# Three of the four sums of down-projection weight blocks made during the up stage, and weight loads counted in buffers (hybrid decoder layer, one core)

## The chip, the cores and the metric

One core of a Trainium2 chip runs the kernel. The metric is the device time of one execution in microseconds (us); the median of 3 runs stands for a kernel. The engines are called TensorE (PE, matmuls; PEld is its weight load), VectorE (DVE), ScalarE (ACT), GpSimd (POOL) and SyncE (SP, which issues transfers). A transfer that adds into its destination (an accumulate) is issued by GpSimd.

## The reference, cut to what matters

One decoder layer on 512 tokens of width 1024, in float32: attention and a gated short convolution, merged and projected, and then a feed-forward part. Only the last line concerns the change:

```python
x = x + mixed @ w_out
h = rms_norm(x, norm2_g)
return x + jnp.square(jax.nn.relu(h @ w_up)) @ w_down     # w_up 1024 x 4096, w_down 4096 x 1024
```

## The kernel before

Every weight comes from DRAM in blocks of 128 x 1024 (512 KB). `Weights` holds a plan of them in the order of use. Each block is split into a high and a low part (ScalarE copies into `w_hi`, line 87; VectorE subtracts into `w_lo`, line 89), in four steps of half a block's high, half a block's low, and again. Each product is then three matmuls (`mm3`, lines 252 to 254): high by high, low by high, high by low. The splits are put into the program a few blocks ahead of their use: `split_step` is called between matmuls, two blocks ahead in an up stage and three in a down stage. There are 3 buffers for raw blocks (`w_raw`) and 4 for split ones. SyncE, which issues the loads (line 65), works in program order: a load whose buffer is still read holds up all loads behind it. `load_to(self.ns + 2)` runs after each split and loads up to the plan's second entry after the next.

The feed-forward part runs in four groups of 1024 inner channels. An up stage computes 8 tiles of 128 channels by 512 tokens (8 x 24 matmuls) and squares them (`act_evac`, lines 881 to 903: ScalarE 888 and 895, VectorE 889 and 896 to 902). A down stage (`st_down`, lines 931 to 990) multiplies them by the group's part of `w_down` with seven products of halves in place of eight (Strassen's scheme in Winograd's form). The scheme needs blocks of `w_down` and sums of them; block (kh, nh) is row half kh and column half nh, each in two pieces c = 0 and 1 of 512 KB:

| product | weights, in order of use | where they lie before |
|---|---|---|
| 1 | (0,0) | staged tile `st_a` |
| 2 | (1,0) | `w_raw` |
| 3 | (0,0) + (0,1) | `st_a` after an accumulate |
| 4 | (1,1) + (0,0) + (0,1) | staged tile `st_e` |
| 5 | (1,1) | `w_raw` |
| 6 | (0,1) + (1,1) | staged tile `st_b` |
| 7 | the 4th + (1,0) | `st_e` after another accumulate |

So a down stage has 14 chunks (7 products by 2 pieces) of 12 matmuls, 4 splits steps of a later block between them. After the second piece of a product VectorE adds its accumulators into `x1` (line 941); where the next product accumulates in the same PSUM tile, TensorE waits for that add. A plan entry is a DRAM block, or a pair of functions: one that gives a staged tile, and one that is called after its split and issues what comes next for that tile: a load of the next group's block (SyncE, line 142) or an accumulate (GpSimd, line 146). In the order before:

- after the split of `st_a` as (0,0): accumulate (0,1) onto `st_a`, then accumulate `st_a` onto `st_e`;
- after its second split: load the next group's (0,0) into it, which has to wait until the accumulate that reads `st_a` has ended;
- after the first split of `st_e`: accumulate (1,0) onto it; after its second: load the next group's (1,1);
- after the split of `st_b`: load the next group's (0,1) and accumulate (1,1) onto it.

As pairs take up entries of the plan but no raw buffer, two entries ahead is often less than three loads ahead there. In the first up stage the tiles are loaded once, and `st_b` is accumulated (lines 914 to 916).

Of the kernel before, what the change touches and what calls it, by code (L numbers as in the profile page):

```python
# [6 lines left out]
F32 = mybir.dt.float32  # L7
F32R = mybir.dt.float32r
AF = mybir.ActivationFunctionType
ALU = mybir.AluOpType  # L10
# [3 lines left out]
P = 128  # L14
# [21 lines left out]
class Weights:  # L36
# [16 lines left out]
    def dram(self, n):  # L53

        src = self.flat[self.at : self.at + P * n].rearrange("(p n) -> p n", p=P)
        self.at += P * n
        return src

    def load_to(self, i):
        while self.nl <= min(i, len(self.plan) - 1):  # L60
# [5 lines left out]
                self.loaded[self.nl] = t[:, :n]  # L66
            self.nl += 1

    def split_step(self):

        nc, k = self.nc, self.ns
        if k >= len(self.plan):
            return
        e = self.plan[k]
        if self.step == 0:
            self.load_to(k)
            if isinstance(e, tuple):
                self.loaded[k] = e[0]()
            hi = self.hl.tile([P, WMAX], F32R, name="w_hi", tag="w_hi")
            lo = self.hl.tile([P, WMAX], F32R, name="w_lo", tag="w_lo")  # L80
            self.parts[k] = (hi, lo)
        hi, lo = self.parts[k]
        t = self.loaded[k]
        n = t.shape[1]
        v = slice(0, n // 2) if self.step < 2 else slice(n // 2, n)
        if self.step % 2 == 0:
            nc.scalar.activation(hi[:, v], t[:, v], AF.Copy)  # L87
        else:
            nc.vector.tensor_tensor(lo[:, v], t[:, v], hi[:, v].bitcast(F32), ALU.subtract)  # L89
        self.step = (self.step + 1) % 4  # L90
        if self.step == 0:
            self.loaded.pop(k)
            self.ns += 1
            if isinstance(e, tuple):
                e[1]()
            self.load_to(self.ns + 2)

    def split_to(self, i):
        while self.ns <= min(i, len(self.plan) - 1):
# [7 lines left out]
def layer(tc, flat, sizes, x, cst, wck, wcv, g1, g2, out):  # L107
    nc = tc.nc
# [25 lines left out]
    W.plan = [W.dram(n) for n in sizes]  # L134


    st = {}

    def st_load(g, what, c):
        src = {"a": (0, 0), "b": (0, 1), "e": (1, 1)}[what]  # L140
        t = st["pool"].tile([P, 1024], F32, name=f"st_{what}{c}", tag=f"{what}{c}")
        nc.sync.dma_start(t, down_src(g, *src, c))
        st[what, c] = t

    def st_add(t, src):
        nc.gpsimd.dma_start(t, src, accum_op=ALU.add)  # L146

    def st_loads(g, c, what):
        if g < 4:
            st_load(g, what, c)  # L150
            if what == "b":
                st_add(st["b", c], down_src(g, 1, 1, c))

    def down_src(g, kh, nh, c):
        return down_blocks[g][kh, nh][:, c * 1024 : (c + 1) * 1024]

    def st_plan(g):


        def first(c):  # L160
            st_add(st["a", c], down_src(g, 0, 1, c))
            st_add(st["e", c], st["a", c])

        def tile_of(what, c, done):
            return (lambda: st[what, c], done)

        def both(f):
            return [f(c) for c in range(2)]

        out = both(lambda c: tile_of("a", c, lambda: first(c)))  # L170
        out += both(lambda c: down_src(g, 1, 0, c))
        out += both(lambda c: tile_of("a", c, lambda: st_loads(g + 1, c, "a")))
        out += both(lambda c: tile_of("e", c, lambda: st_add(st["e", c], down_src(g, 1, 0, c))))
        out += both(lambda c: down_src(g, 1, 1, c))
        out += both(lambda c: tile_of("b", c, lambda: st_loads(g + 1, c, "b")))
        out += both(lambda c: tile_of("e", c, lambda: st_loads(g + 1, c, "e")))
        return out

    down_blocks = []
    for g in range(4):  # L180
        W.plan += [W.dram(1024) for _ in range(8)]
        down_blocks.append({(kh, nh): W.dram(2048) for kh in range(2) for nh in range(2)})
        W.plan += st_plan(g)
# [415 lines left out]
    def u_scores(u, c):  # L599

        h, br = units[u]
        n = P * (c + 1)
        a, b = (S - n, S + P) if c == 0 else (S, S + n) if br else (S - n, S)
        t = slice(c * P, (c + 1) * P)
        ps = ps_sc.tile([P, S], F32, name="sc", tag="sc")
        for k, ks in enumerate((KS1, KS2)):
            nc.tensor.matmul(  # L607
                ps[:, : b - a], QS[h][:, t], ks[h // 4][:, a:b], start=k == 0, stop=k == 1
            )

        def soft(v, src):
            p = p_of(v, c)
            mn, sm = (nst[:, v % 4, k, c : c + 1] for k in range(2))
            dd = C_DD + S - n if c == 0 or units[v][1] else C_DR
            nc.vector.tensor_tensor_reduce(
                p, src, cs[:, dd : dd + n], -(2.0 ** -(h + 1)), 3.0e38,
                op0=ALU.add, op1=ALU.min, accum_out=mn,
            )
            later(1, lambda: nc.scalar.activation(
                p, p, AF.Exp, scale=-1.0, bias=mn, accum_out=sm  # L620
            ))

        if c == 0:
            for k in range(2):
                soft(u + k, ps[:, k * P : (k + 1) * P])
        else:
            soft(u, ps[:, :n])

        def norm(c0):
            r = nst[:, u % 4, 1, c0 : c0 + 2]  # L630
            nc.vector.tensor_scalar(r, r, 1.0e-30, None, op0=ALU.max)
            nc.vector.reciprocal(r, r)
            nc.vector.tensor_tensor(r, r, gates[:, c0 : c0 + 2, (br + 1) * NH + h], ALU.mult)
            for k in (c0 + 1, c0):
                nc.gpsimd.tensor_scalar(
                    p_of(u, k), p_of(u, k), nst[:, u % 4, 1, k : k + 1], 1.0,
                    op0=ALU.mult, op1=ALU.mult,
                )

        if c == 2 or c == br:  # L640
            later(3, lambda: norm(2 if c == 2 else 0))
# [4 lines left out]
    def u_trans(u, grp):  # L646
        br = units[u][1]
        pth, ptl = ptb[u % 2]
        pt = ps_tr.tile([P, S], F32, name="ptu", tag="tr")
        n = 0  # L650
        for j in grp:
            for c in range(j, NT):
                k = j if br else c - j
                nc.tensor.transpose(  # L654
                    pt[:, n : n + P], p_of(u, c)[:, k * P : (k + 1) * P], ident
                )
                n += P
        at = slice(PT_AT[grp[0]], PT_AT[grp[0]] + n)
        nc.scalar.activation(pth[:, at], pt[:, :n], AF.Copy)
        later(1, lambda: nc.vector.tensor_tensor(  # L660
            ptl[:, at], pt[:, :n], pth[:, at].bitcast(F32), ALU.subtract
        ))

    def u_pv(u, js):
        h, br = units[u]
        g = h // 4
        pth, ptl = ptb[u % 2]
        if br == 0 and js[0] == 0:
            pv_now[0] = ps_pv.tile([P, S], F32, name="pv", tag="pv")
        pv = pv_now[0]  # L670
        for j in js:
            at, q0 = (0, 256) if j == 3 else (PT_AT[j], j * P)
            w = S - q0
            v = V[:, j, br * 2 + g, :, :].rearrange("p a d -> p (a d)")
            nc.tensor.matmul(  # L675
                pv[:, q0:], v, pth[:, at : at + w], start=(br == 0 and j == 0), stop=False
            )
            nc.tensor.matmul(  # L678
                pv[:HD, q0:], v[:, :HD], ptl[:, at : at + w], start=False, stop=False
            )  # L680
# [18 lines left out]
    for u in range(nu + 2):  # L699
        s = [lambda c=c, u=u: u_scores(u, c) for c in (3, 2, 1, 0)[: 4 - u % 2]] if u < nu else []  # L700
        t, f = [], []
        if 1 <= u <= nu:
            t = [lambda g=g, v=u - 1: u_trans(v, g) for g in ((3, 2), (1,), (0,))]
        if u >= 2:
            f = [lambda j=j, v=u - 2: u_pv(v, j) for j in ((0, 1), (2, 3))]
# [62 lines left out]
    for n in range(NKO):  # L768
        sg = []
        for i in range(2):  # L770
            ps = tile_t(ci, (xh, xl), NKO, ps_t)
            s = gp.tile([P, S], F32, name=f"sg{i}", tag=f"sg{i}")
# [138 lines left out]
        up.tile([P, NP, 7, 256], F32R, name="ul"),  # L911
        None,
    ]
    for c in range(2):
        for what in "abe":
            st_loads(0, c, what)
    pss = [ps_acc.tile([P, S], F32, name="acc", tag="acc") for _ in range(4)]
    for half in range(2):
        for f in range(4):
# [188 lines left out]
```

## Time and profile before

| | us |
|---|---|
| median of 3 runs | 868.86 (865.09 to 871.91) |
| the profiled execution | 869.74 |
| its span, first to last instruction | 868.0 |
| first up stage, up to its last matmul | 484 to 535 |
| the four down stages begin at | 535.1, 630.0, 725.8, 821.5 |

Times in the rows are us from the start of the span, with the length of a piece in the second column of a timeline; brackets hold the idle time of the engine just before an instruction and what ended it. Matmuls overlap, so the length of one is more than its share of the time. TensorE's granted clock is 1.00 at 2.4 GHz and 0.50 at 1.2 GHz.

### The profile page before, as it was taken

The numbers are of one execution on the slowest core, as the hardware profiler recorded it, in microseconds if no ns is written. First come the engines' busy times: TensorE is split into PE (matmuls) and PEld (weight loads), VectorE is DVE, ScalarE is ACT, GpSimd is POOL, SyncE is SP. The second block draws the span as 40 slices with busy tenths as digits, with TensorE's granted clock in tenths as the row PEclk, the third lists the DMA queues.
The fourth block names the chain that finished last, engine by engine and source line by source line (L and its number), as shares of the span: only waits on it lengthen the run. The fifth ranks groups of instructions, "written<-read, shape, count | busy, mean of one in ns | idle before, by whom it ended". The sixth has DMA issues, their size and how long they took to land.

```text
span 868.0 us, 10722 instructions
## 1 busy us (share of the span) xinstructions
PE 822.8 (95%) x3941; PEld 678.5 (78%) x3941; DVE 512.0 (59%) x1026; ACT 358.4 (41%) x735; POOL 91.8 (11%) x138
## 2 busy tenths in 40 slices
PE   5999999999999999999999998889998899889998
PEld 4898778888887888888888986668876787768876
DVE  6677977666665544333435566555665367455684
ACT  5455455545544423232324444233443244323451
POOL 0101642221221000000000001100010001100020
PEclk9999999999999999999999999989999999999999
DMA  8213121212121242323262563873176724782372
GB/s 318 83 52 122 49 73 49 74 49 74 52 70 41 82 134 85 105 89 97 98 243 72 188 177 51 187 220 107 66 145 193 220 72 74 170 265 98 73 164 79
DMA packets 29861, 101.17 MB, mean 117 GB/s; under 512 B 3441, under 2 KB 3825, under 8 KB 29809
## 3 DMA queue, kind: packets, MB, share of 16 engines
q1 hardware_dynamic: 24336, 81.02, 28.0%
q0 software_dynamic: 4608, 16.78, 10.6%
q10 hardware_dynamic: 864, 2.69, 0.9%
q8 instruction: 31, 0.51, 0.2%
q14 instruction: 22, 0.17, 0.1%
HBM read 94.18 MB, written 2.10 MB: 111 GB/s over the span
## 4 chain that ended last, share of the span: by engine, by line
PE 60%; issue 20%; DMA 9%; DVE 6%; ACT 3%; POOL 1%; SPq 0%; POOLq 0%; ACTq 0%; DVEq 0%
PE acc L252 16%; PE acc L254 16%; PE acc L253 16%; DMA w_raw<-w_flat 5%; DMA st_e<-st_a 2%; DVE w_lo L89 2%; PE ptu L654 2%; PE sc L607 2%; PE dacc L253 2%; PE dacc L252 2%; PE dacc L254 2%; DMA st_b<-w_flat 1%; PE pv L678 1%; PE pv L675 1%; POOL st_a L146 1%
## 5 line engine op out<-in xcount | busy, mean ns | idle before, releaser
L89 DVE TENSOR_TENSOR w_lo<-w_raw,w_hi 128x512 fp32r<-128x512 f32 (+2 forms) x252 | 158.2, 661 | 120.9 <-ACT w_hi L87 120.7
L87 ACT ACTIVATE w_hi<-w_raw 128x512 fp32r<-128x512 f32 (+2 forms) x252 | 137.6, 594 | 91.7 <-DMA w_raw<-w_flat 82.3
L252 PE MATMUL acc<-xh,w_hi 128*128 128x512 f32 x336 | 137.4, 409 | 0.0
L254 PE MATMUL acc<-xh,w_lo 128*128 128x512 f32 x336 | 131.5, 391 | 0.0
L253 PE MATMUL acc<-xl,w_hi 128*128 128x512 f32 x336 | 131.3, 391 | 0.0
L252 PE MATMUL dacc<-w_hi,uh 128*128 128x512 f32 (+1 forms) x228 | 95.3, 418 | 23.1 <-DVE x L941 18.9
L252 PE MATMUL acc<-hh,w_hi 128*128 128x512 f32 (+1 forms) x288 | 105.6, 367 | 2.1 <-DVE G L889 1.8
L253 PE MATMUL acc<-hl,w_hi 128*128 128x512 f32 (+1 forms) x288 | 105.4, 366 | 0.3 <-DVE hl L246 0.3
L254 PE MATMUL acc<-hh,w_lo 128*128 128x512 f32 (+1 forms) x288 | 105.3, 365 | 0.0
L253 PE MATMUL dacc<-w_lo,uh 128*128 128x512 f32 (+1 forms) x228 | 94.9, 416 | 3.4 <-DVE w_lo L89 3.4
L254 PE MATMUL dacc<-w_hi,ul 128*128 128x512 f32 (+1 forms) x228 | 93.9, 412 | 0.0
L252 PEld LDWEIGHTS dacc<-w_hi,uh 128*128 128x128 f32 x228 | 46.6, 204 | 37.3 <-ACT w_hi L87 26.6
L254 PEld LDWEIGHTS acc<-xh,w_lo 128*128 128x128 f32 x336 | 63.1, 188 | 14.1
L252 PEld LDWEIGHTS acc<-xh,w_hi 128*128 128x128 f32 x336 | 63.2, 188 | 11.9 <-issue 3.3
L253 PEld LDWEIGHTS acc<-xl,w_hi 128*128 128x128 f32 x336 | 63.3, 189 | 8.0
L252 PEld LDWEIGHTS acc<-hh,w_hi 128*128 128x128 f32 x288 | 54.3, 189 | 11.3 <-DVE G L889 2.2
L253 PEld LDWEIGHTS acc<-hl,w_hi 128*128 128x128 f32 x288 | 54.3, 189 | 9.2 <-DVE hl L246 0.5
L254 PEld LDWEIGHTS acc<-hh,w_lo 128*128 128x128 f32 x288 | 54.3, 189 | 8.8
L253 PEld LDWEIGHTS dacc<-w_lo,uh 128*128 128x128 f32 x228 | 46.7, 205 | 14.3 <-DVE w_lo L89 4.6
L254 PEld LDWEIGHTS dacc<-w_hi,ul 128*128 128x128 f32 x228 | 46.6, 204 | 10.0
L896 DVE TENSOR_TENSOR ul<-G,uh 128x768 fp32r<-128x768 f32 (+1 forms) x32 | 34.9, 1092 | 32.7 <-ACT uh L895 32.7
L895 ACT ACTIVATE uh<-G 128x768 fp32r<-128x768 f32 (+1 forms) x32 | 30.5, 953 | 56.0 <-DVE G L902 41.8
(202 smaller groups left out, 1308.4 us busy)
## 6 DMA issues: line engine op xcount, KB each, us to landing
w_raw<-w_flat SPq DMA_DIRECT2D x110, 512.0 KB, 3.6
st_a<-w_flat SPq DMA_DIRECT2D x8, 512.0 KB, 6.1
st_b<-w_flat SPq DMA_DIRECT2D x8, 512.0 KB, 5.9
st_e<-w_flat SPq DMA_DIRECT2D x8, 512.0 KB, 10.7
st_b<-w_flat POOLq DMA_DIRECT2D x8, 512.0 KB, 9.7
st_a<-w_flat POOLq DMA_DIRECT2D x8, 512.0 KB, 6.4
st_e<-st_a POOLq DMA_DIRECT2D x8, 512.0 KB, 5.0
st_e<-w_flat POOLq DMA_DIRECT2D x8, 512.0 KB, 7.9
```

The costliest lines, as they stand in the source:

```text
L87: nc.scalar.activation(hi[:, v], t[:, v], AF.Copy)
L89: nc.vector.tensor_tensor(lo[:, v], t[:, v], hi[:, v].bitcast(F32), ALU.subtract)
L146: nc.gpsimd.dma_start(t, src, accum_op=ALU.add)
L252: nc.tensor.matmul(ps, a[0], b[0], start=start, stop=False, **kw)
L253: nc.tensor.matmul(ps, a[0], b[1], start=False, stop=False, **kw)
L254: nc.tensor.matmul(ps, a[1], b[0], start=False, stop=stop, **kw)
L607: nc.tensor.matmul(ps[:, : b - a], QS[h][:, t], ks[h // 4][:, a:b], start=k == 0, stop=k == 1)
L654: nc.tensor.transpose(pt[:, n : n + P], p_of(u, c)[:, k * P : (k + 1) * P], ident)
L675: nc.tensor.matmul(pv[:, q0:], v, pth[:, at : at + w], start=(br == 0 and j == 0), stop=False)
L678: nc.tensor.matmul(pv[:HD, q0:], v[:, :HD], ptl[:, at : at + w], start=False, stop=False)
L895: nc.scalar.activation(hi, G[:, v, :], AF.Copy)
L896: nc.vector.tensor_tensor(lo, G[:, v, :], hi.bitcast(F32), ALU.subtract)
```

## The change

Block (0,0) of the first product is now a raw block of its own (two loads of 512 KB more a group). `st_a`, `st_b` and `st_e` of a group are loaded during the down stage before, as their tiles come free, and three of the four sums are made from there on: (0,1) onto `st_a` after the first use of `st_e`, then (1,1) onto `st_b` and `st_a` onto `st_e` after the last use of `st_e`. Only (1,0) onto `st_e` stays in its own down stage; it is issued for both pieces together. Loads into `w_raw` go on until three unsplit blocks are loaded or being loaded, whatever pairs lie between.

```diff
+    def load_ahead(self):
+
+        while self.nl < len(self.plan) and (
+            isinstance(self.plan[self.nl], tuple)
+            or sum(not isinstance(self.plan[i], tuple) for i in range(self.ns, self.nl)) < 3
+        ):
+            self.load_to(self.nl)
...
-            self.load_to(self.ns + 2)
+            self.load_ahead()
...
+    def st_add(g, what, src):
+
+        if g < 4:
+            for c in range(2):
+                s = st[src, c] if src == "a" else down_src(g, *src, c)
+                nc.gpsimd.dma_start(st[what, c], s, accum_op=ALU.add)
+
+    def st_first(g):
+
+        st_add(g, "b", (1, 1))
+        st_add(g, "e", "a")
...
+        def dram(kh, nh):
+            return [down_src(g, kh, nh, c) for c in range(2)]
+
+        def tile_of(what, then=None):
+            def done(c):
+                if what == "e" and then:
+                    if c:
+                        st_add(g, "e", (1, 0))
+                        st_add(g + 1, "a", (0, 1))
+                else:
+                    st_load(g + 1, c, what)
+                    if what == "e" and c:
+                        st_first(g + 1)
+
+            return [(lambda c=c: st[what, c], lambda c=c: done(c)) for c in range(2)]
+
+        return (
+            dram(0, 0) + dram(1, 0) + tile_of("a") + tile_of("e", True)
+            + dram(1, 1) + tile_of("b") + tile_of("e")
+        )
...
-    for c in range(2):
-        for what in "abe":
-            st_loads(0, c, what)
+    for what in "abe":
+        for c in range(2):
+            st_load(0, c, what)
+    st_add(0, "a", (0, 1))
+    st_first(0)
```

SyncE's queue from the first group's down stage to the second's, before: `w_raw` is a raw block, `st_a`, `st_b` and `st_e` with a number are the staged tiles (two pieces each) of the second group.

```order
L65 DMA w_raw<-w_flat 128x1024 x3
L142 DMA st_a_4785<-w_flat 128x1024
L142 DMA st_a_4806<-w_flat 128x1024
L65 DMA w_raw<-w_flat 128x1024 x2
L142 DMA st_b_4909<-w_flat 128x1024
L142 DMA st_b_4931<-w_flat 128x1024
L65 DMA w_raw<-w_flat 128x1024
L142 DMA st_e_4955<-w_flat 128x1024
L65 DMA w_raw<-w_flat 128x1024
L142 DMA st_e_4978<-w_flat 128x1024
L65 DMA w_raw<-w_flat 128x1024 x8
```

The same stretch of SyncE's queue now (line 152 is the load of a staged tile):

```order
L65 DMA w_raw<-w_flat 128x1024 x8
L152 DMA st_a_4795<-w_flat 128x1024
L152 DMA st_a_4816<-w_flat 128x1024
L65 DMA w_raw<-w_flat 128x1024 x2
L152 DMA st_b_4921<-w_flat 128x1024
L152 DMA st_b_4942<-w_flat 128x1024
L152 DMA st_e_4963<-w_flat 128x1024
L152 DMA st_e_4984<-w_flat 128x1024
L65 DMA w_raw<-w_flat 128x1024 x12
```

Before, the x3 ahead of `st_a` are the first up stage's last block and the two pieces of (1,0), and the x2 behind it the pieces of (1,1). Now the x8 hold the first up stage's last block, (0,0), (1,0) and (1,1) with two pieces each, and the first block of the next up stage; the x2 are that stage's second and third block.

GpSimd's queue from the first group's accumulates on, before (staged tiles 4314 to 4326 are the first group's, those above the second's):

```order
L146 DMA st_b_4316<-w_flat 128x1024
L146 DMA st_b_4323<-w_flat 128x1024
L146 DMA st_a_4314<-w_flat 128x1024
L146 DMA st_e_4319<-st_a_4314 128x1024
L146 DMA st_a_4321<-w_flat 128x1024
L146 DMA st_e_4326<-st_a_4321 128x1024
L146 DMA st_e_4319<-w_flat 128x1024
L146 DMA st_e_4326<-w_flat 128x1024
L146 DMA st_b_4909<-w_flat 128x1024
L146 DMA st_b_4931<-w_flat 128x1024
```

And now:

```order
L160 DMA st_a_4314<-w_flat 128x1024
L160 DMA st_a_4316<-w_flat 128x1024
L160 DMA st_b_4318<-w_flat 128x1024
L160 DMA st_b_4320<-w_flat 128x1024
L160 DMA st_e_4322<-st_a_4314 128x1024
L160 DMA st_e_4324<-st_a_4316 128x1024
L160 DMA st_e_4322<-w_flat 128x1024
L160 DMA st_e_4324<-w_flat 128x1024
L160 DMA st_a_4795<-w_flat 128x1024
L160 DMA st_a_4816<-w_flat 128x1024
```

Now six accumulates of the first group stand ahead of its down stage instead of two, the two onto `st_e` in the down stage follow each other, and the next group's onto `st_a` come right behind them.

## Rows read from the trace of the kernel before

**Rows 1.** The page, its first part: an engine's busy time, share of the span, instructions.

```profile
PE 822.8 (95%) x3941; PEld 678.5 (78%) x3941; DVE 512.0 (59%) x1026; ACT 358.4 (41%) x735; POOL 91.8 (11%) x138
```

**Rows 2.** Waits by releaser, 535 to 822 us: total us, times, longest.

```profile
ACT w_hi L87 <- DMA w_raw<-w_flat: 66.0, 14, 7.1
...
PE dacc L252 <- DVE x L941: 18.4, 6, 4.1
...
PE dacc L252 <- ACT w_hi L87: 3.1, 3, 1.0
PE dacc L253 <- DVE w_lo L89: 2.5, 3, 0.8
```

**Rows 3.** Busy time by stretch: length, busy by engine, granted clock, share of transfers, GB/s.

```profile
core 0: us, PE busy (x) PEld busy (x) DVE busy (x) ACT busy (x) POOL busy (x), PEclk, DMA share, GB/s
484.00:535.10 51.10, 48.70 (x311) 43.84 (x310) 32.37 (x54) 21.00 (x37) 2.75 (x3) 1.00 0.53 158
...
552.00:569.00 17.00, 14.18 (x56) 11.30 (x55) 7.81 (x13) 6.23 (x12) 0.86 (x1) 0.90 0.68 160
569.00:586.00 17.00, 14.10 (x55) 11.16 (x54) 7.40 (x13) 3.87 (x7) 1.73 (x2) 0.90 0.94 279
...
647.00:664.00 17.00, 14.74 (x58) 11.69 (x58) 7.44 (x13) 6.62 (x12) 0.86 (x1) 0.90 0.65 157
664.00:682.00 18.00, 13.90 (x55) 11.02 (x54) 8.34 (x15) 3.52 (x7) 1.73 (x2) 0.91 0.91 268
...
743.00:760.50 17.50, 14.77 (x58) 11.77 (x57) 7.72 (x13) 6.69 (x12) 0.86 (x1) 0.90 0.64 154
760.50:778.00 17.50, 13.94 (x55) 11.02 (x54) 8.27 (x15) 3.45 (x6) 1.73 (x2) 0.90 0.93 275
828.00:839.00 11.00, 10.02 (x36) 7.88 (x37) 9.37 (x16) 5.60 (x12) 1.73 (x2) 0.84 0.76 152
839.00:856.00 17.00, 17.00 (x77) 14.08 (x76) 12.91 (x20) 7.29 (x13) 0.86 (x1) 1.00 0.56 131
```

**Rows 4.** The chain that ended last, in order of time: start, us, what.

```profile
642.18 6.12 DMA st_e<-st_a
648.37 0.33 SPq L142
648.75 0.45 SPq L65
649.25 10.31 DMA w_raw<-w_flat
659.67 0.64 ACT w_hi L87
...
761.86 6.75 DMA w_raw<-w_flat
...
770.08 0.61 DVE x L941
770.82 0.47 PE dacc L252
```

**Rows 5.** From issue to landing, loads of line 65 (`w_raw`).

```profile
DMA to landing us min/median/max: 2.4/3.5/14.1
```

**Rows 6.** The page, its third part: transfer queues, packets, MB, share of 16 engines.

```profile
q1 hardware_dynamic: 24336, 81.02, 28.0%
q0 software_dynamic: 4608, 16.78, 10.6%
```

**Rows 7.** Timelines of SyncE, ScalarE and TensorE in the first up stage.

```profile
504.69 10.88 SPq L65 DMA_DIRECT2D w_raw<-w_flat  x3
...
514.19 1.14 ACT L87 ACTIVATE w_hi<-w_raw 128x512 fp32r<-128x512 f32 x2
...
524.10 0.50 PE L252 MATMUL acc<-hh,w_hi 128*128 128x512 f32 x1 [1.81 <-DVE G L889]
```

**Rows 8.** Timelines of GpSimd and ScalarE in the fourth group.

```profile
840.54 0.86 POOL L146 DMA_DIRECT2D st_e<-w_flat  x1 [2.12 <-DVE w_lo L89]
...
838.29 1.15 ACT L87 ACTIVATE w_hi<-st_e 128x512 fp32r<-128x512 f32 x2 [2.59 <-DMA st_e<-st_a]
...
850.25 1.16 ACT L87 ACTIVATE w_hi<-st_e 128x512 fp32r<-128x512 f32 x2 [1.57 <-PE dacc L254]
852.97 1.15 ACT L87 ACTIVATE w_hi<-st_e 128x512 fp32r<-128x512 f32 x2 [1.56 <-PE dacc L254]
```

**Rows 9.** From issue to landing, accumulates of line 146 (all three tiles).

```profile
DMA to landing us min/median/max: 4.5/7.5/10.1
```

**Rows 10.** From issue to landing, loads of line 142 (staged tiles).

```profile
DMA to landing us min/median/max: 3.5/6.7/13.3
```

More of the change, by code (lines that the diff above doesn't have):

```diff
@@ L137, in layer, with st_load @@
     st = {}
-    def st_load(g, what, c):
+    def st_load(g, c, what):
         src = {"a": (0, 0), "b": (0, 1), "e": (1, 1)}[what]
[L141 to L148, printed above, removed]
-        if g < 4:
-            st_load(g, what, c)
-            if what == "b":
-                st_add(st["b", c], down_src(g, 1, 1, c))
+        if g < 4:
+            t = st["pool"].tile([P, 1024], F32, name=f"st_{what}{c}", tag=f"{what}{c}")
+            nc.sync.dma_start(t, down_src(g, *src, c))
+            st[what, c] = t
+    def st_add(g, what, src):
[6 more added lines that the diff above has]
+        st_add(g, "e", "a")
     def down_src(g, kh, nh, c):
@@ L157, in st_plan @@
     def st_plan(g):
[L160 to L177, printed above, removed]
+        def dram(kh, nh):
[15 more added lines that the diff above has]
+        )
     down_blocks = []
```

## The prediction

> **What bounds the kernel now.** I read the page first: TensorE is busy 95% of the span [rows 1], so only what stops it or slows its clock counts. Then its waits by releaser, in the stretch of the first three groups: three lines hold nearly all of it. Three times it waits 1.0 us for a high part and three times 0.8 us for a low part (5.6 us together), and six times it waits for line 941, VectorE's adding of a finished product into `x1`: 18.4 us, the longest 4.1 [rows 2]. Then the busy time by stretch, two stretches a group [rows 3]: what TensorE misses is 2.82 and 2.90 us in the first group, 2.26 and 4.10 in the second, 2.73 and 3.56 in the third, 18.37 us in all, so these stretches hold exactly those six waits. In each of the six its granted clock is 0.90 or 0.91 on the mean. In the fourth group, 839 to 856 us, the same products run with 17.00 us busy of 17.00 at 1.00: no wait, no low clock. The fourth group has no next group to load for.
>
> Why VectorE is late stands in the chain that ended last [rows 4]. In the second group: the accumulate of `st_a1` into `st_e1` ends after 6.12 us; only then may SyncE issue the load that overwrites `st_a1` (648.37, line 142); behind it in SyncE's queue stand the loads of block (1,1) into `w_raw` (648.75), the second of which takes 10.31 us; ScalarE splits it at 659.67. The adds of line 941 stand behind the low part of that split in VectorE's queue, so TensorE, which needs the accumulator read before it may reuse it, waits. The second wait of a group is the same at another place: the first weight block of the next up stage is loaded at 761.86 only, for 6.75 us, and the add at 770.08 and the product at 770.82 come behind its split. Both waits are late transfers, not late arithmetic.
>
> **The change part by part.** On TensorE, VectorE and ScalarE the order of the work stays; only the source of the first two splits of a group turns from `st_a` into `w_raw`. That moves nothing there.
>
> Removed, first wait. By the SyncE order before, two loads of `st_a` with a wait for an accumulate stand ahead of the two raw loads of block (1,1). Now a raw load is issued whenever fewer than three lie unsplit, so block (1,1) goes out as soon as a buffer comes free: its first half once the second half of (0,0) is split, at the very end of the up stage, its second once the first half of (1,0) is split. TensorE's short waits at the start of a down stage are for that very split, at the third of fourteen chunks; the second half of (1,1) is split beside the seventh. Four chunks lie between, of 12 products and 2.65 us each (17.00 us hold 77 products [rows 3]): 10.6 us. A raw load takes 3.5 us at the median and 14.1 at the longest [rows 5]. At the median there are 7 us to spare; the 14.1 would be 3.5 late, but comes from the crowd of the down stage, which the change thins out. And the `st_a` load no longer waits long: the accumulate of `st_a` into `st_e` now ends in the up stage. Worth 2.82 + 2.26 + 2.73 = 7.81 us.
>
> Removed, second wait. The next up stage's first block is now the raw load right after block (1,1), ahead of the `st_a` loads, so it lies ready from the first third of the down stage; the next two follow as block (1,1) is split, half a stage before use. Worth 2.90 + 4.10 + 3.56 = 10.56 us.
>
> Removed with them, the low clock: (1 - granted clock) times length, in the six stretches, is 1.70 + 1.70 + 1.70 + 1.62 + 1.75 + 1.75 = 10.22 us [rows 3]. It follows each wait and not the work: the fourth group shows 1.00 over the same work. If the waits shrink to a fraction but don't go, this term may stay whole, since the short waits at the start of each down stage also go with a lowered clock (the 1.9 us wait of the fourth group, and 0.84 in the 828 to 839 stretch [rows 3]).
>
> Untouched: those short waits at the start of the four down stages. They are ScalarE's, which splits the third block behind the squaring of the last up tile; the order there is the same.
>
> Added, transfers. Eight raw loads of 512 KB (blocks (0,0), which before were split in `st_a` itself, are now loaded twice). All hardware-queue loads, 81.02 MB, take 28.0% of 16 engines' span, so 512 KB costs 868 x 0.28 x 0.524 / 81.02 = 1.57 us of all engines; an accumulate costs 868 x 0.106 / 32 = 2.87 us [rows 6]. So 8 x 1.57 = 12.6 us more in a span whose engines are idle for more than half. Cover: all of it beside matmuls; without the cover at most 1.57 us a load.
>
> Moved, accumulates. In each group the accumulate of (0,1) onto `st_a`, and of `st_a` onto `st_e`, go from the down stage into the stage before; they have some 50 us there and cost nothing. For the first group they stand beside the loads at the start of the first up stage: four more accumulates, 11.5 us, and 1.57 for one more load, in a stretch of 51.10 us with a share of 0.53, 27.1 us [rows 3]. That makes 40 of 51 us: it fits on the whole, though the first 25 us will be full. What stands there: SyncE's load of the eighth up block issued at 504.69 and split at 514.19 [rows 7]. Bounds: nothing, if it lands as before; 11.5 us late plus a lowered clock (1.7), if all four accumulates come ahead of it and it had landed only just in time. I take nothing: the load has 9.5 us, over the median by 6, and the split shows no wait for a transfer [rows 7].
>
> The Trainium skill (DMA: Bandwidth & Descriptors, "Issuing engines are not separate DMA queues") speaks against this: transfers of all issuers run on the same 16 engines and interleave, so GpSimd's queue is no separate road. The trace agrees as far as it goes: in the stretch of the second wait of group one the share is 0.94 [rows 3] and loads are slow there. By that rule the loads of the start lengthen, which is the rival "crowd at the start" below; by the rows there is room for that.
>
> The one accumulate that stays in the down stage is block (1,0) onto `st_e`, between its two uses. Now both halves are issued together after the second half of `st_e` is split, with the next `st_a` accumulates behind them in GpSimd's queue. The fourth group shows the timing: second half split at 838.29 after waiting 2.59 us for a transfer, so it would be split at 835.7 and the accumulates issued near 838 and 839 (the wait of GpSimd's second one before ended at 840.54); the two halves are split at 850.25 and 852.97 [rows 8]. Accumulates land in 4.5 to 10.1 us, 7.5 at the median [rows 9]: 848 and 849 at the longest, before both uses. If one is served after the other, each at 10.1, the second comes at 858.2, 5.2 us late. I take no wait, being nearer to the median. No end below nothing: nothing else waits for these.
>
> **Sum.** Against the profiled execution, 869.74 us: 869.74 - 7.81 - 10.56 - 10.22 = 841.15. That execution lies 0.88 above the median of the runs shown, 868.86; so 840.3.
>
> **Rivals.**
> The second sum comes late. For it: four accumulates now follow each other in one queue. Against it: the loads beside them are spread out, and group four had them 3 us apart without a wait. Price: half of the 5.2 us and the lowered clock, 2.6 + 1.7 = 4.3 a group, three groups: 840.3 + 12.9 = 853; with the whole 5.2, 861.
> Crowd at the start: 11.5 + 1.7 = 13.2 once: 853.5. Against it: the share of 0.53, and 9.5 us between issue and use.
> The change doesn't do all that it says: the raw loads of the next group still come late, behind `st_a` in SyncE's queue, and only the first wait goes: 840.3 + 10.56 + 1.70 + 1.62 + 1.75 = 856. Against it: the order, in which one of them now stands ahead of `st_a`; and `st_a` itself has nothing to wait for.
> Slower than before: GpSimd's queue serves in series at the pace of the slowest staged load, 13.3 us [rows 10]. Then the second half of the second sum, issued behind the first at 838, lands at 838 + 26.6 = 864.6 in the terms of group four, 11.6 us after its use; with the clock 13.3 us for each of the groups 1 to 3, 39.9: 880. It outweighs the gain from 28.6 / 3 - 1.7 = 7.8 us late. Against it: no accumulate took more than 10.1.
>
> **How the numbers follow.** Forecast 0.74 (836 to 846); second sum late 0.10; crowd at the start 0.08; only the first wait gone 0.05; slower 0.03. A measurement of this kernel can tell about 1% from no change, 8.7 us. The first four lie under 860.2, save for their far ends, for which I move 0.05 to "within 1%": faster 0.92, same 0.05, slower 0.03. The range goes from 836 (a short wait at a stage's start that shrinks too) to 855, which takes in the forecast and the two rivals at 853; it leaves out the last two and the far ends.
>
> **What would show it.** Right: in groups one to three TensorE has no waits for line 941 above 1 us; the three periods from down stage to down stage shrink from 95 to 86 us; the clock there falls once a group, not three times; ScalarE's 66.0 us of waits for `w_raw` [rows 2] fall to a few. The first up stage keeps its wait of 1.81 us [rows 7]. Wrong: splits of `st_e` that wait for an accumulate in the second half of a down stage, or a wait of TensorE before 530 us that is longer than 1.81.

## The result, and the profile after

The changed kernel takes 839.51 us (838.57 to 841.31); the kernel before took 869.28 beside it. The ratio is 0.9664, 95% interval 0.9622 to 0.9706: faster. The forecast was 840.3. The profiled execution took 841.31 with a span of 839.5 us, 28.5 less than before.

Waits of TensorE by releaser in the changed kernel, longest totals first (total us, times, longest); line 267 is the old 252, 268 the old 253, 904 the old 889 and 958 the old 941:

```profile
PE ptr L258 <- DVE x L248: 9.5, 1, 9.5
PE dacc L267 <- ACT w_hi L95: 4.2, 4, 1.0
PE dacc L268 <- DVE w_lo L97: 3.4, 4, 0.8
PE acc L267 <- DVE G L904: 1.8, 1, 1.8
...
PE dacc L267 <- DVE x L958: 0.5, 1, 0.5
```

The six waits for line 941, 18.4 us in [rows 2], are gone; the 0.5 is at the end of the last group, where the kernel before has it too. Of ScalarE's waits for raw loads, 66.0 us in [rows 2], none is left between 535 and 800 us. The short waits at the start of the four down stages are as they were. The busy time by stretch, from short wait to short wait (columns as in [rows 3]):

```profile
484.00:537.60 53.60, 51.20 (x315) 45.72 (x314) 33.38 (x56) 22.04 (x39) 5.35 (x6) 0.97 0.73 213
544.25:629.92 85.67, 83.78 (x360) 68.65 (x360) 56.71 (x91) 36.20 (x61) 6.99 (x8) 0.98 0.62 172
629.92:713.97 84.05, 82.17 (x360) 67.49 (x360) 56.52 (x91) 36.20 (x61) 6.99 (x8) 1.00 0.63 176
713.97:799.64 85.67, 83.78 (x360) 68.61 (x361) 56.70 (x91) 36.22 (x61) 6.99 (x8) 0.98 0.62 172
```

The reader is to see the first column: a period of a group is 84 to 86 us. The same stretches of the kernel before:

```profile
541.76:636.69 94.93, 87.33 (x361) 70.69 (x361) 55.48 (x91) 36.09 (x61) 6.95 (x8) 0.95 0.53 142
636.69:732.47 95.78, 87.54 (x360) 70.70 (x360) 55.53 (x91) 35.97 (x61) 6.95 (x8) 0.95 0.53 143
732.47:828.14 95.67, 87.50 (x360) 70.80 (x360) 55.53 (x91) 35.96 (x61) 6.95 (x8) 0.95 0.56 149
```

The three periods are 9.26, 11.73 and 10.00 us shorter, 30.99 in all; some 2.5 us are given back ahead of the first down stage, of which 0.8 is the wait at the kernel's start (9.5 for 8.7) and most of the rest a low clock in the first up stage (0.97 for 1.00). TensorE misses 1.89 us a period in place of 7.60 to 8.24, 18.4 us in all: the idle time that was forecast to go. The rest, 12.6 us, is the clock, at 0.98, 1.00 and 0.98 on the mean in place of 0.95.

Accumulates got slower, raw loads did not. From issue to landing, accumulates (line 160), then raw loads (line 65), of the changed kernel; [rows 9] had 4.5/7.5/10.1 and [rows 5] 2.4/3.5/14.1:

```profile
DMA to landing us min/median/max: 6.9/11.5/16.9
...
DMA to landing us min/median/max: 2.5/3.7/11.1
```

### The profile page after: what moved, and what is told of

Same layout as the page of the kernel before. It is cut to its first block, busy times and chain, and to the rows that moved or that the text cites. A ratio compares the mean times of both kernels' runs of the same rounds, so it can differ in the third digit from the quotient of the medians.

```text
span 839.5 us, 10750 instructions
## 1 busy us (share of the span) xinstructions
PE 811.4 (97%) x3941; PEld 671.6 (80%) x3941; DVE 515.7 (61%) x1026; ACT 359.2 (43%) x735; POOL 92.0 (11%) x138
## 4 chain that ended last, share of the span: by engine, by line
PE 86%; DVE 8%; ACT 3%; issue 2%; DMA 1%; POOL 0%; SPq 0%; DVEq 0%; ACTq 0%; POOLq 0%
PE acc L267 21%; PE acc L269 20%; PE acc L268 20%; PE dacc L268 6%; PE dacc L269 5%; PE dacc L267 5%; PE ptu L669 2%; PE sc L622 2%; DVE w_lo L97 1%; ACT uh L910 1%; PE pv L693 1%; PE pv L690 1%; PE ptr L258 1%; DVE ul L911 1%; DMA g1b<-g 1%
## 5 line engine op out<-in xcount | busy, mean ns | idle before, releaser
L97 DVE TENSOR_TENSOR w_lo<-w_raw,w_hi 128x512 fp32r<-128x512 f32 (+2 forms) x268 | 168.5, 663 | 77.5 <-ACT w_hi L95 77.4
L95 ACT ACTIVATE w_hi<-w_raw 128x512 fp32r<-128x512 f32 (+2 forms) x268 | 146.7, 596 | 51.4 <-PE dacc L269 30.7
L267 PE MATMUL dacc<-w_hi,uh 128*128 128x512 f32 (+1 forms) x228 | 90.2, 395 | 4.7 <-ACT w_hi L95 4.2
L268 PE MATMUL dacc<-w_lo,uh 128*128 128x512 f32 (+1 forms) x228 | 90.3, 396 | 3.4 <-DVE w_lo L97 3.4
L269 PE MATMUL dacc<-w_hi,ul 128*128 128x512 f32 (+1 forms) x228 | 89.9, 394 | 0.0
L267 PEld LDWEIGHTS acc<-hh,w_hi 128*128 128x128 f32 x288 | 54.7, 190 | 11.5 <-DVE G L904 2.2
L267 PEld LDWEIGHTS dacc<-w_hi,uh 128*128 128x128 f32 x228 | 44.1, 193 | 15.5 <-ACT w_hi L95 5.9
L268 PEld LDWEIGHTS dacc<-w_lo,uh 128*128 128x128 f32 x228 | 43.9, 193 | 13.7 <-DVE w_lo L97 4.6
L634 ACT ACTIVATE p<-p,nst 128x512 f32<-128x512 f32 (+2 forms) x48 | 29.6, 616 | 56.4 <-DVE nst L630 55.1
```

The source lines that it names most:

```text
L267: nc.tensor.matmul(ps, a[0], b[0], start=start, stop=False, **kw)
L268: nc.tensor.matmul(ps, a[0], b[1], start=False, stop=False, **kw)
L269: nc.tensor.matmul(ps, a[1], b[0], start=False, stop=stop, **kw)
L634: later(1, lambda: nc.scalar.activation(p, p, AF.Exp, scale=-1.0, bias=mn, accum_out=sm))
```

## The experiments

The kernel before has a median of 862 to 869 us on the chips used here, the changed one 838.7 to 839.9. So kernels are compared where they ran on the same chip.

**The counted loads alone, and beside the whole change.** To the kernel before only this is added:

```diff
+    def load_ahead(self):
+        ...
-            self.load_to(self.ns + 2)
+            self.load_ahead()
```

> The kernel before with the loads counted in buffers, and nothing else: the sums stay in the down stage. Theory (both waits are raw loads that SyncE issues too late): blocks (1,1) and the next up stage's first block now stand ahead of the st_a loads, so both waits of a group and their low clock go although the accumulates still stand in the down stage: 841 us (838 to 846). Rival (the chain of accumulates in the down stage is what makes VectorE late, and only its move ahead helps): the first wait of each group stays, 7.81 us and 5.1 of clock: 854 or more.

839.52 us, 0.9735 of the kernel before (0.9708 to 0.9763), which took 863.29 there. The changed kernel was then run beside it:

> The loads counted in buffers alone, once more, beside the whole change on one chip. Theory (the early sums bring nothing): within 0.5% of the next run. Rival (the early sums bring what the slower second sums cost, or more): 1% or more above or below it.

> The whole change on the chip of ahead_again, to be set against it: a ratio of 0.966 to 0.974 to the kernel before by either theory.

839.41 us, 0.9725 (0.9698 to 0.9753), and 838.71 us, 0.9730 (0.9695 to 0.9764): the same. The rival falls: the sums may stay in the down stage. What the loads did shows in TensorE's waits of the first of these runs (260 is the old 252):

```profile
PE ptr L251 <- DVE x L241: 8.5, 1, 8.5
PE dacc L260 <- ACT w_hi L95: 4.2, 4, 1.0
PE dacc L261 <- DVE w_lo L97: 3.4, 4, 0.8
```

Of the waits for VectorE's add only the 0.5 us at the end is left. SyncE's timeline (start, us, what) of the first down stage shows why; line 150 is a load of a staged tile:

```profile
543.64 1.53 SPq L65 DMA_DIRECT2D w_raw<-w_flat  x2
546.64 8.98 SPq L150 DMA_DIRECT2D st_a<-w_flat  x2
559.04 2.13 SPq L65 DMA_DIRECT2D w_raw<-w_flat  x2
```

The second `st_a` load still has to wait for its accumulate, 8.98 us for the pair, as in the kernel before (8.66 there, from 546.68). But the raw loads TensorE needs next stand ahead of it, so nothing that matters is behind, and no wait of TensorE comes of it.

**The early sums alone.** The changed kernel, with one line as before:

```diff
-            self.load_ahead()
+            self.load_to(self.ns + 2)
```

> The changed kernel with loads counted in plan entries as before: the sums are early, but block (1,1) and the next up stage's first block are loaded late in the order. Theory: block (1,1) stands behind st_a loads that no longer wait for an accumulate, so the first wait goes; the next up stage's first block still stands behind the st_b loads, issued 5 us before its split, so the second wait stays in part: 840 + 3 x (1 to 3.5 + 1.7) = 848 to 856. Rival (accumulates are what matters): as the changed kernel, 839 to 842.

854.41 us, 0.9897 (0.9858 to 0.9936): some 9 of 24 us, and less than the theory gave (a ratio of 0.976 to 0.985 by its times). TensorE waits for VectorE's adds three times a run plus the 0.5 at the end:

```profile
PE dacc L267 <- DVE x L958: 8.9, 4, 3.9
```

All three are second waits of their groups, 2.05, 2.48 and 3.86 us. The chain that ended last shows the first of them:

```profile
564.43 0.33 SPq L152
564.82 6.49 DMA w_raw<-w_flat
571.42 0.64 ACT w_hi L95
572.08 0.69 DVE w_lo L97
572.77 0.61 DVE x L958
573.51 0.47 PE dacc L267
```

It reads like the end of the chain in [rows 4]: a staged load ahead in SyncE's queue, the next up stage's block behind it, its split, the add behind the split, the product. The early sums free `st_a` soon enough for the first wait, but not for the second.

**Raw load first.** The kernel before, with two statements exchanged:

```diff
-            if isinstance(e, tuple):
-                e[1]()
             self.load_to(self.ns + 2)
+            if isinstance(e, tuple):
+                e[1]()
```

> The kernel before with two lines of the split's end exchanged: the raw load is issued ahead of what a pair issues, so the first half of (1,1) stands ahead of the second st_a load and not behind it. Theory: the first wait of a group is that position in SyncE's queue and nothing else: it goes (7.81 and 5.1 us), the second stays: 856 us (853 to 860). Rival (SyncE's order is not the cause, transfers are slow by crowding): within 1% of the kernel before, 866 to 870.

847.29 us, 0.9828 (0.9798 to 0.9858), 16 us off the kernel before. No transfer, tile or accumulate is saved here, so the rival (crowding) falls: SyncE's order alone is worth two thirds of the change. SyncE's first down stage:

```profile
546.30 0.33 SPq L142 DMA_DIRECT2D st_a<-w_flat  x1
546.72 0.38 SPq L65 DMA_DIRECT2D w_raw<-w_flat  x1
554.27 0.33 SPq L142 DMA_DIRECT2D st_a<-w_flat  x1
554.69 0.38 SPq L65 DMA_DIRECT2D w_raw<-w_flat  x1
```

The first half of (1,1) now goes out at 546.72, not at 555.44 behind the second `st_a` load. The first waits are down to under 0.6 us each, and of the waits for VectorE's add these are left:

```profile
PE dacc L252 <- DVE x L941: 4.7, 4, 1.9
```

The theory had the second waits stay whole; they shrank too, to 0.49, 1.88 and 1.83 us, as each next block stands one staged load further forward. That is 6.4 us less than the 10.56 of before, and the granted clock around the last two is 1.00. The gain was 16 us where 13 were expected. The two don't add up closely, and no run shows why: the kernel before was not profiled on this chip, where it takes 863.29 us and not 868.86.

**The second sum last.** In the changed kernel the order of two issues is exchanged:

```diff
-                        st_add(g, "e", (1, 0))
                         st_add(g + 1, "a", (0, 1))
+                        st_add(g, "e", (1, 0))
```

> The changed kernel with GpSimd's two accumulates of the next group's st_a put ahead of the two of (1,0) onto st_e, so the second sum lands last of four. Theory (the second sum has 5 us to spare or more, and four in a row land within some 16 us): 0 to 3 us more than the changed kernel, 839 to 843. Rival of the prediction (the second sum is close to late): each of groups one to three waits 2.6 us or more with a low clock behind it, 852 or more.

852.11 us, 0.9871 (0.9828 to 0.9915), beside 839.52 for the counted loads alone and 838.71 for the changed kernel on that chip: 12.6 to 13.4 us lost, and the theory falls. The chain that ended last in the first group:

```profile
555.49 0.87 POOL st_a L160
556.57 16.04 DMA st_e<-w_flat
573.25 2.70 ACT w_hi L95 x5
576.01 0.77 PE dacc L267
576.78 0.43 PE dacc L268
```

The accumulate takes 16.04 us, the splits come in a burst and TensorE waits 4.18 us; from then until 582 us matmuls start 0.43 us apart instead of 0.23. The third group has such a wait of 3.20 us, the second none: 7.4 us of waits in the profiled run, which took 849.64. How the rest up to the median of 852.11 came about was not profiled. So the last of four accumulates in a row does take some 16 us, as expected; the wrong step was to let the one that is needed first be that last one.

**Three blocks ahead, with and without the early sums.** What was left over at the start of a down stage was tried as a version of its own: in the up stages (in the first of them from the fifth tile on) the splits run three blocks ahead.

```diff
-            act_evac(tile_t(ci + f, (hh, hl), NKO, ps_t), act, f)
+            ps = ps_t.tile([P, S], F32, name="acc", tag="acc")
+            tile_t_into(ps, ci + f, (hh, hl), NKO, ahead=3)
+            act_evac(ps, act, f)
```

> The changed kernel once more, on the chip and beside the runs of the next two, so that they can be set against it. Theory and rivals alike: a ratio of 0.966 to 0.974 to the kernel before.

> The changed kernel with splits three blocks ahead in the up stages from the fifth tile on (two in the changed kernel), so that the third block of a down stage is split before the squaring of the last up tile and not behind it. Theory (the four short waits at the start of the down stages are this order on ScalarE and VectorE, and nothing else): 4 x 1.88 us and three low clocks of 1.7 go, 12.6 us off the changed kernel, 0.985 of it. Rival (the split only takes the place of the squaring, whose result the second chunk needs): the waits move to the second chunk, 1.2 us each with the clock as before, 2 to 3 us off.

> The kernel before with loads counted in buffers and with splits three blocks ahead in the up stages, the sums left in the down stage. Theory (the early sums bring nothing): as three_ahead within 0.5%. Rival (with the short waits gone the down stage starts 1.9 us sooner against its accumulates, and the sums made there come late): a wait for the split of st_e in the third product's place, 2 us or more a group with a low clock, 5 us or more above three_ahead.

On one chip, with the kernel before at 868.3 us: the changed kernel 839.93, 0.9678 (0.9656 to 0.9701); with three blocks ahead 825.11, 0.9506 (0.9484 to 0.9528); three ahead and counted loads without early sums 825.29, 0.9506 (0.9484 to 0.9529). Both beat the changed kernel by 14.6 to 14.8 us, somewhat more than the 12.6 expected. The waits of TensorE in the version with early sums:

```profile
PE ptr L258 <- DVE x L248: 8.5, 1, 8.5
PE acc L267 <- DVE G L904: 1.8, 1, 1.8
```

No line for `w_hi` or `w_lo` is left, and the busy time by stretch is full at full clock through three groups:

```profile
534.00:617.00 83.00, 83.00 (x368) 68.73 (x367) 56.27 (x91) 36.33 (x60) 6.94 (x8) 1.00 0.63 177
617.00:700.00 83.00, 83.00 (x368) 68.76 (x367) 56.81 (x91) 36.31 (x61) 6.97 (x8) 1.00 0.65 182
700.00:784.00 84.00, 84.00 (x372) 69.60 (x371) 57.24 (x92) 37.58 (x62) 6.97 (x8) 1.00 0.65 182
```

The rival (the wait moves to the second chunk) falls. And the early sums bring nothing here either, though the accumulates of a down stage meet a stage that starts sooner.

## Why the prediction was right, point by point

**The two late loads.** Right, and shown: exchanging two statements takes the first waits, counting loads takes both, and the sums have little part in the second (alone they leave 8.4 of 10.56 us). What the forecast gave to them, 18.37 us of idle time, is what went. One reading was off, which changed no number. It put the first wait of the second group down to the second load of (1,1), which takes 10.31 us and is split at 659.67 [rows 4]. TensorE's wait had ended by then; it ended with the add behind the split of the first piece:

```profile
656.21 1.15 ACT L87 ACTIVATE w_hi<-w_raw 128x512 fp32r<-128x512 f32 x2 [6.65 <-DMA w_raw<-w_flat]
...
657.48 0.68 DVE L941 TENSOR_TENSOR x<-x,dacc 128x512 f32<-128x512 f32 x1
...
658.30 0.47 PE L252 MATMUL dacc<-w_hi,uh 128*128 128x512 f32 x1 [2.26 <-DVE x L941]
```

The first piece stands behind the same two `st_a` loads, so the cause is the one that was named.

**Which part of the change does it.** The prediction's step "and the `st_a` load no longer waits long: the accumulate of `st_a` into `st_e` now ends in the up stage" was named beside the loads as if it were needed. It is not: with the loads counted, that load waits 8.98 us for its pair and the time is the same. The title's part of the change, three sums made early, is worth nothing measurable beside the counted loads, and some third of the gain without them.

**The low clock.** The size was right: 10.22 us were forecast over six waits, and (1 - granted clock) times span is 17.4 us in the profile before (0.980 of 868.0) and 6.7 in the one after (0.992 of 839.5). The places were right in part. Right behind the short waits of the second group the clock stayed at 1.00, and the first up stage had a fall that it had not had, behind the unchanged wait of 1.81 us. TensorE's timeline in the changed kernel:

```profile
525.02 0.66 PE L267 MATMUL acc<-hh,w_hi 128*128 128x512 f32 x1 [1.81 <-DVE G L904]
525.47 0.63 PE L268 MATMUL acc<-hl,w_hi 128*128 128x512 f32 x1
525.90 0.63 PE L269 MATMUL acc<-hh,w_lo 128*128 128x512 f32 x1
...
629.92 0.50 PE L267 MATMUL dacc<-w_hi,uh 128*128 128x512 f32 x1 [1.04 <-ACT w_hi L95]
631.26 0.50 PE L268 MATMUL dacc<-w_lo,uh 128*128 128x512 f32 x1 [0.84 <-DVE w_lo L97]
631.61 0.40 PE L269 MATMUL dacc<-w_hi,ul 128*128 128x512 f32 x1
631.85 0.40 PE L267 MATMUL dacc<-w_hi,uh 128*128 128x512 f32 x1
```

The starts are 0.43 us apart in the first stretch (1.2 GHz) and 0.24 in the second (2.4 GHz). "The clock there falls once a group" held on the count of four, one fall of which lies in the first up stage, and none in the second group. The count is luck in part: another profile of the changed kernel has 1.00 in the first up stage and behind the short waits of the third group, and three falls.

**The crowd at the start.** Forecast to fit: 40 of 51 us, a share of 0.78; measured over 484 to 537.6 us, 0.73. The wait in the first up stage is 1.81 us as before [rows 7], so the price was nothing, as taken. The low clock behind that wait is not the crowd's either: from 484 to 538 us two more profiles of the changed kernel show 1.00, and one of the counted loads alone, without the early accumulates, 0.97.

**The total.** The profiled executions lie 28.4 us apart, where 28.59 were forecast. So close a number is luck in part: the three periods gave 2.4 us more than that, and 2.5 were given back ahead of the first down stage, 0.8 of them by the wait at the kernel's start, which the forecast didn't have and which is 8.2 to 9.5 us from profile to profile.

**The second sum.** No wait came, as taken, but the bound doesn't hold for every accumulate. "Accumulates land in 4.5 to 10.1 us" was used for accumulates in a row too, and all those of the changed kernel take 6.9 to 16.9, 11.5 at the median. The accumulates of [rows 9] stood alone or in twos. For the second sum itself the forecast held: its accumulates land in 7.9 us at the median, as in the kernel before, and in 12.9 where they stand behind the two onto `st_a`. The pages of the changed kernel and of that experiment:

```profile
st_e<-w_flat POOLq DMA_DIRECT2D x8, 512.0 KB, 7.9
...
st_e<-w_flat POOLq DMA_DIRECT2D x8, 512.0 KB, 12.9
```

What kept the second sum in time is that it is issued ahead of the next group's `st_a` accumulates; one place later it costs 12.6 to 13.4 us. The rival at 853 had the right price, 12.9, for a kernel one line away, though in that kernel's profile two longer waits make it up and not one in each of three groups. With the loads counted alone the accumulates stay fast:

```profile
DMA to landing us min/median/max: 4.6/7.1/11.0
```

So the part of the change that moves the sums made them slow, and not the raw loads that now come sooner.

**The Trainium skill's rule** (DMA: Bandwidth & Descriptors, "Issuing engines are not separate DMA queues") spoke against the change, and the runs agree in part: the accumulates took longer (11.5 us for 7.5 at the median), the raw loads hardly (3.7 for 3.5). Whether the shared engines or GpSimd's one queue made them slower is not shown. It changed no time, as what grew longer was not waited for.

## What to carry to other kernels

Where one queue issues both transfers that must wait for a buffer and transfers that are needed soon, look first at their order in the queue: here an exchange of two statements gave two thirds of the gain, and a count in real buffers instead of plan entries gave all of it, with no transfer saved. Split a change into its parts before keeping all of it: the larger part of this one (new accumulate order, 4 MB more loads) was worth nothing beside the smaller. And where an engine's short waits recur at each stage's start, read whose work stands ahead of the one it waits for: splitting one block earlier was worth 14.8 us more.

## What was not expected of the hardware

The same wait lowers the clock at one time and not at another. In the changed kernel the periods behind the short waits of 1.04 and 0.84 us are 85.67, 84.05 and 85.67 us with granted clocks of 0.98, 1.00 and 0.98 on the mean; the waits are alike to 0.01 us, so a fall of the clock costs 1.62 us here. In a second profile of the same kernel the periods are 84.05, 85.70 and 85.66: the one that is spared is another.
